# Second products of the attention scores and the filter features over 128 partitions instead of 64

## The chip, the cores and the metric

The kernel runs on one core of a Trainium2 chip. The time is device microseconds of one execution; several executions were timed, and one more view of an execution, the profile, tells what each engine did and when. Engines are named as the profile names them: PE is TensorE's matmul, PEld its weight load, DVE VectorE, ACT ScalarE, POOL GpSimd, SP SyncE, which here issues all DMAs.

## What is computed

One layer of a two-branch encoder over two inputs, the prompt (1024 tokens) and the sample (512 tokens), both 1024 channels wide:

```python
def encoder_layer(x, ...):
    h = rmsnorm(x, norm_g)
    z = h @ w_in
    ...
    # branch 1: long convolution with a filter that a small network makes
    hy_in = short_conv(hy_in, conv_w, conv_b)
    x0, x1, vv = jnp.split(hy_in, 3, axis=-1)
    kfilt = hyena_filter(L, f_w1, f_b1, f_fr1, f_w2, f_b2, f_fr2, f_w3)
    y_hy = x0 * long_conv(x1 * vv, kfilt, hy_bias)
    y_hy = rmsnorm(y_hy, on_hy) * jax.nn.silu(hy_gate)
    # branch 2: attention in a window of 8 rows by 16 columns of a grid 64 wide
    q = rmsnorm(q.reshape(B, L, N_HEADS, HEAD_DIM), qn_g)      # 8 heads of 64
    k = rmsnorm(k.reshape(B, L, N_HEADS, HEAD_DIM), kn_g)
    y_att = neighbourhood_attention(q, k, v, rpb)
    y_att = rmsnorm(y_att, on_att) * jax.nn.silu(att_gate)
    return x + jnp.concatenate([y_hy, y_att], axis=-1) @ w_out

def hyena_filter(L, w1, b1, fr1, w2, b2, fr2, w3):
    ...
    h = jnp.sin(fr1 * (z @ w1 + b1))
    h = jnp.sin(fr2 * (h @ w2 + b2))       # L x 64, the features
    h = h @ w3                              # 64 -> 1024 channels
    h = h * jnp.exp(-t01 * jnp.abs(deltas))
    ...
```

All is float32. TensorE works on a rounded form, so every exact operand is held as a rounded part (hi) and what is left (lo), and a product is made of hi x hi, hi x lo and lo x hi.

## The kernel before, in words

**Stages.** First the prompt's x is normed and turned channel-major (`x_norm`, `x_turn`), and the features of the filters are made (`filters_mlp`, L166 its matmuls). Then the prompt's q, k and v are projected (`qk_proj` and `v_proj`, matmuls at L405), and alongside `k_phase` makes the filters of both groups and transforms them (L568, L569, then L461 to L463). Then comes the prompt's long convolution (`hyena`, with projections at L392), then the attention of the prompt alongside the projections and the convolution of the sample, then the output product (`out_part`, L1111) alongside the attention of the sample, and last the rest of the outputs.

**Order.** Generators are woven step by step in a fixed plan, some with a priority; the order on each engine is then set by the scheduler of the language, which runs a timeline of its own over the program while it is built. Any edit can so move instructions far from it. Each engine takes its queue in order; all DMAs stand in one queue, SP's. Room is given out by pools. A pool that is closed hands its room to the next ones on the same side, and an instruction that writes there waits for the last reader of the tile before.

**Filter products.** A feature and its weight each have 64 values, so a tile of 128 partitions holds two sorts of them. `hm` (features) has, for direction d, hi on the partitions of d and lo on the other 64; `w3[d]` has hi of the weights on both halves. One matmul over 128 partitions (L568) therefore makes hi x hi + lo x hi. The missing hi x lo is a second matmul, over the 64 partitions of d alone (L569), against `w3[2]`, which holds lo of direction d on the partitions of d. Two such pairs fill a bank, and `k_phase` multiplies it by the decay `dec` (into `xk`, VectorE). `dec` is loaded through three buffers, three loads ahead.

**Scores.** Per pair of heads `load_pair` fills `kst` (k: hi on the head's half of the partitions, lo on the other), `qhh` (q: hi on both halves) and `qlo` (lo of q of the two heads, each on its half, in one tile). In `soft` L994 multiplies `qhh` by `kst` over 128 partitions, and L995 the head's half of `qlo` by the same half of `kst`, into the same bank. There are 64 such pairs for the prompt (half of them with 360 columns, half with 480) and 32 for the sample (360 columns). VectorE adds the table and finds the smallest (L998, `mx`), ScalarE takes exponentials (L1002), and the weights are scaled, turned (L1020) and multiplied by the values (L1029).

**Around it.** `issue_w` splits the weights into hi (L365) and lo (L366, on GpSimd). `gap` is a tile that is never used: it holds room free between the sample's projections and the pools of the sample's hyena, so that the first outputs (`ops0`, `ops1`, `acc0`, `first`) find room while that hyena still runs. `oo` (L1123, ScalarE) is the tile of the pool `first`, through which the outputs of the prompt's second half pass. W (copied at L671) is the spectrum of a block in `long_conv`.

Of the kernel before, what the change touches and what calls it, by code (L numbers as in the profile page):

```python
# [49 lines left out]
class Kernel:  # L50
# [6 lines left out]
    # ---------------------------------------------------------------- helpers  # L57
# [28 lines left out]
    def psum(self, side, keep=0, **banks):  # L86
        """Share the banks of one side out anew, but for its first keep pools: tag -> number of banks."""
# [11 lines left out]
    # ------------------------------------------------------------------ setup  # L99
    def setup(self):  # L100
# [27 lines left out]
        # DRAM scratch  # L128
# [11 lines left out]
    def mlp_setup(self, fl, mp):  # L140
        io = self.io
        self.hm, self.z, self.w12 = {}, {}, []
        self.w3 = [fl.tile([P, HW], F32R, name=f"w3{n}") for n in ("f", "b", "lo")]
# [12 lines left out]
    def filters_mlp(self, G, mp):  # L156
        nc = self.nc
        tag = "" if G.nseg > 1 else "_s"
        w1, w2 = self.w12
        h = self.z[G.name]  # L160
        for layer, (w, b, fr) in enumerate(((w1, "b1", "fr1"), (w2, "b2", "fr2"))):
            nxt = None if layer else mp.tile([P, G.L], F32, name=f"h1_{G.name}")
            for s in range(G.nseg):
# [3 lines left out]
                arg = mp.tile([P, 512], F32, name="arg" + tag, bufs=G.nseg)  # L167
                self.ts(arg, ps, self.v[b], ALU.add, self.v[fr], ALU.mult)
                n = mp.tile([P, 512], F32, name="n" + tag, bufs=G.nseg)
# [16 lines left out]
    def stack(self, out, src):  # L186
        """The halves of the partitions of src, split: hi in their own place and lo on the other half."""
        for d in range(2):
            r, o = slice(d * 64, d * 64 + 64), slice(64 - d * 64, 128 - d * 64)
            self.nc.scalar.copy(out=out[d][r], in_=src[r])  # L190
            self.sub(out[d][o], src[r], f32(out[d][r]))

    def w3_load(self, pool):
        """The last weights of the filters: per half of the partitions hi on both halves, and lo in its place."""
        raw = pool.tile([P, HW], F32, name="w3", bufs=1)
        self.dma(raw, self.io["w3"])
        for d in range(2):
# [3 lines left out]
            self.sub(self.w3[2][r], raw[r], f32(self.w3[d][r]))  # L201

    def rsqrt(self, pool, ss, n, scale, name):
        """(ss * scale + eps) ** -0.5 for a [P, n] tile."""
# [13 lines left out]
    # ------------------------------------------------------------ input norm  # L218
    def x_norm(self, G, xp, ahead):
        """The rows of x, scaled by their rms."""  # L220
# [18 lines left out]
    def x_turn(self, G, hps):  # L239
        """Channel-major copies of the normed x, split into hi and lo."""  # L240
# [12 lines left out]
    def x_pre(self, G, pool):  # L253
        """Channel-major copies of the normed x, split into hi and lo, to scratch."""
# [39 lines left out]
    # --------------------------------------------------------------- weights  # L294
    def steps(self, what):
        """The pieces of the weights that each step of a generator takes."""
# [19 lines left out]
    def merge(ns, spans):  # L316
        """The order in which generators of ns[i] steps take turns, each spread evenly over its span."""
# [3 lines left out]
    def plan(self, phases):  # L321
        """phases: lists of (names of chained generators, span, priority).  Sets the order of the weights."""
# [9 lines left out]
    def weave(self, *gens):  # L332
        """Trace the generators of the next phase in turns."""
# [10 lines left out]
    def fetch_w(self):  # L344
        """Load the next [P, 1024] piece."""
# [8 lines left out]
    def issue_w(self):  # L354
        """Split the next piece into two units of (hi, lo) [P, 512]; the piece behind it is on its way."""
# [13 lines left out]
    def take_w(self, key):  # L369
        """The next unit of piece key; pieces behind it are fetched as far as there is room."""  # L370
# [8 lines left out]
    def proj_ch(self, G, *gis):  # L379
        """128 output channels of each granule of gis, channel-major: per granule a list of psum [P, 512].  # L380
        The granules take turns in each segment of tokens."""
# [13 lines left out]
    def proj_tok(self, gi, hi, lo, nt):  # L395
        """256 output columns, token-major, for nt (<=8) token tiles.  Returns list of psum [P, 4, 256]."""
# [12 lines left out]
    # ----------------------------------------------------------------- hyena  # L409
    def conv(self, out, pss, ci):  # L410
        """short convolution along the free axis; ci = channel block (0..11)."""
# [13 lines left out]
    def dft_load(self, t, src, pool, tag):  # L425
        """src (DRAM) -> t [P, n, 128], rounded, through the room of a tag of pool."""
# [4 lines left out]
    def dft_mats(self, pool, src, fs, stage, tags):  # L431
        """The class matrices of the 128-point transforms: per class ((cos hi, lo), (sin hi, lo)).
# [101 lines left out]
    def k_phase(self, fp, between):  # L534
# [20 lines left out]
        for _ in range(3):  # L555
            fetch()
# [845 lines left out]
```

## Time and profile before

| | us |
|---|---|
| median of 3 runs | 1100.63 |
| lowest, highest | 1098.63, 1104.17 |
| span of the profiled execution, first to last instruction | 1101.3 |
| PE busy in it | 1030.7 |
| DVE busy in it | 824.4 |
| ACT busy in it | 561.1 |
| POOL busy in it | 539.9 |

The profiled execution lies inside the range of the timed ones. Busy time is the time in which at least one instruction of the engine is under way. On PE the matmuls overlap, so a row's duration is longer than the distance to the next one; the distance between two starts tells what a matmul takes of the engine. A form `64*128 64x360` is a matmul over 64 partitions, with 128 columns of weights and 360 moving columns.

### The profile page before, as it was taken

How to read it: one execution, taken by the hardware profiler on the slowest of the kernel's cores; microseconds unless marked ns; L12 is line 12 of the kernel's file. 1: busy time of each engine (PE TensorE's matmuls, PEld its weight loads, DVE VectorE, ACT ScalarE, POOL GpSimd, SP SyncE). 2: the span in 40 equal slices, each digit the busy share in tenths (PEclk: the TensorE clock that was granted, in tenths of full speed). 3: DMA queues.
4: the chain of work that ended last, by engine and by line, in shares of the span. 5: the costliest groups of instructions: out<-in, count | busy, mean ns of one | idle time of the engine just before them, and what ended most of it. 6: DMA issues, size and time to landing. Idle time of an engine off the chain costs nothing. (4 is left out here: it accounts for less than half of the span.)

```text
span 1101.3 us, 18549 instructions
## 1 busy us (share of the span) xinstructions
PE 1030.7 (94%) x6492; PEld 895.6 (81%) x6492; DVE 824.4 (75%) x2098; ACT 561.1 (51%) x1223; POOL 539.9 (49%) x480
## 2 busy tenths in 40 slices
PE   3999898998999999999898999999999999899998
PEld 2888887987888878787786887888777798798898
DVE  5988679456148597868768898999886868966874
ACT  6644616444534343443425577667567764564530
POOL 2133636325245474545445645455455564766452
PEclk9999999899999999999999899999999999999999
DMA  9134461645612121122375244445544376966522
GB/s 343 34 122 144 143 207 61 219 150 164 224 39 74 46 79 54 50 72 77 118 227 173 78 129 146 120 141 182 140 129 138 114 243 190 321 203 205 164 76 89
DMA packets 110780, 154.87 MB, mean 141 GB/s; under 512 B 7793, under 2 KB 80315, under 8 KB 109919
## 3 DMA queue, kind: packets, MB, share of 16 engines
q1 hardware_dynamic: 110687, 153.69, 44.3%
q8 instruction: 51, 0.84, 0.3%
q14 instruction: 42, 0.34, 0.1%
HBM read 110.35 MB, written 43.32 MB: 140 GB/s over the span
## 5 line engine op out<-in xcount | busy, mean ns | idle before, releaser
L366 POOL TENSOR_TENSOR wlo<-wraw,whi 128x512 fp32r<-128x512 f32 x160 | 231.5, 1451 | 308.4 <-ACT whi L365 180.7
L392 PE MATMUL bank<-hThi_p,whi 128*128 128x512 f32 x320 | 125.2, 391 | 2.0 <-DVE cx L75 2.0
L392 PE MATMUL bank<-hTlo_p,whi 128*128 128x512 f32 x320 | 125.5, 392 | 0.0
L392 PE MATMUL bank<-hThi_p,wlo 128*128 128x512 f32 x320 | 125.4, 392 | 0.0
L405 PE MATMUL bank<-whi,hThi_p 128*128 128x256 f32 x384 | 110.4, 290 | 2.5 <-ACT qsq L849 2.0
L1111 PE MATMUL bank<-whi,hi 128*128 128x256 f32 x384 | 111.0, 291 | 0.8 <-ACT hi L1090 0.5
L405 PE MATMUL bank<-wlo,hThi_p 128*128 128x256 f32 x384 | 110.8, 291 | 0.0
L1111 PE MATMUL bank<-wlo,hi 128*128 128x256 f32 x384 | 110.0, 288 | 0.0
L1111 PE MATMUL bank<-whi,lo 128*128 128x256 f32 x384 | 109.5, 289 | 0.3 <-POOL lo L63 0.3
L405 PE MATMUL bank<-whi,hTlo_p 128*128 128x256 f32 x384 | 108.1, 289 | 0.0
L450 POOL TENSOR_TENSOR Z<-zc,Z 128x256 fp32r<-128x256 f32 x80 | 69.5, 878 | 49.2 <-ACT Z L449 36.2
L1002 ACT ACTIVATE s_sb<-s_sb,mx 128x360 f32<-128x360 f32 (+1 forms) x96 | 60.4, 629 | 63.6 <-DVE mx L998 63.0
L405 PEld LDWEIGHTS bank<-whi,hThi_p 128*128 128x128 f32 x384 | 74.2, 194 | 4.9 <-ACT qsq L849 2.4
L1111 PEld LDWEIGHTS bank<-whi,hi 128*128 128x128 f32 x384 | 73.4, 191 | 4.1 <-issue 2.1
L405 PEld LDWEIGHTS bank<-wlo,hThi_p 128*128 128x128 f32 x384 | 74.5, 194 | 1.6 <-issue 0.7
L1111 PEld LDWEIGHTS bank<-wlo,hi 128*128 128x128 f32 x384 | 73.6, 192 | 1.6 <-issue 1.6
L1111 PEld LDWEIGHTS bank<-whi,lo 128*128 128x128 f32 x384 | 73.1, 192 | 1.7 <-issue 1.1
L405 PEld LDWEIGHTS bank<-whi,hTlo_p 128*128 128x128 f32 x384 | 73.3, 194 | 1.2 <-issue 0.7
L392 PEld LDWEIGHTS bank<-hThi_p,whi 128*128 128x128 f32 x320 | 60.3, 188 | 14.0 <-DVE cx L75 2.4
L392 PEld LDWEIGHTS bank<-hTlo_p,whi 128*128 128x128 f32 x320 | 60.4, 189 | 11.3
L392 PEld LDWEIGHTS bank<-hThi_p,wlo 128*128 128x128 f32 x320 | 60.3, 188 | 11.3
L392 PE MATMUL bank<-hThi_s,whi 128*128 128x512 f32 x160 | 64.6, 407 | 4.4 <-DVE cvv L75 2.3
(292 smaller groups left out, 3108.4 us busy)
## 6 DMA issues: line engine op xcount, KB each, us to landing
wraw<-in_w_ch_dram SPq DMA_DIRECT2D x40, 512.0 KB
wraw<-in_w_tk_dram SPq DMA_DIRECT2D x24, 512.0 KB
wraw<-in_w_out_dram SPq DMA_DIRECT2D x16, 512.0 KB
V<-v_p SPq DMA_DIRECT2D x32, 240.0 KB
v_p<-vg SPq DMA_DIRECT2D x32, 160.0 KB
K_p<-Kw SPq DMA_DIRECT2D x4, 1088.0 KB
x<-in_x_prompt_dram SPq DMA_DIRECT2D x8, 512.0 KB
dec<-in_dec_p_dram SPq DMA_DIRECT2D x16, 256.0 KB
```

Of the source, the lines that this page charges most:

```text
L366: nc.gpsimd.tensor_tensor(out=lo, in0=r, in1=f32(hi), op=ALU.subtract)
L392: nc.tensor.matmul(ps, lhsT=w, rhs=h[s][:, k], start=(k == 0 and i == 0), stop=(k == KC - 1 and i == 2))
L405: nc.tensor.matmul(pss[t // 2][:, t % 2, :], lhsT=h[t // 4][:, k, t % 4 * P:(t % 4 + 1) * P], rhs=w, start=(k == 0 and i == 0 and t % 2 == ...
L450: nc.gpsimd.tensor_tensor(out=Z[:, 1, 0:2, :], in0=z, in1=f32(Z[:, 0, 0:2, :]), op=ALU.subtract)
L1002: nc.scalar.activation(out=s_sb[:, :n], in_=s_sb[:, :n], func=AF.Exp, bias=mx, scale=-1.0, accum_out=l)
L1111: nc.tensor.matmul(ps[:, j, :], lhsT=h[:, tok], rhs=w, start=(k == 0 and i == 0 and j == 0), stop=(k == 3 and i == 2 and j == 1))
```

## The change

The second matmul of each pair now runs over all 128 partitions. For the filters, lo of the weights has a tile for each direction, with lo on both halves, so that the second matmul makes hi x lo + lo x lo. For the scores, lo of q has a tile for each head, with zeros on the other head's half; these zeros are written once, when the attention opens, by GpSimd, and the tiles are used in turn. The room for the larger tiles is taken elsewhere: the tiles `arg` and `n` of the filters' network share two buffers where the prompt had two and the sample one more of each; `dec` has two buffers and is loaded two ahead; `gap` is 1024 columns smaller. The diff also takes out comments, which moves the line numbers by a few (L995 is L1001 after, L569 is L568, L1111 is L1117).

```diff
@@ mlp_setup
-        self.w3 = [fl.tile([P, HW], F32R, name=f"w3{n}") for n in ("f", "b", "lo")]
+        self.w3 = [fl.tile([P, HW], F32R, name=f"w3{n}") for n in ("f", "b", "lof", "lob")]
@@ filters_mlp
-        tag = "" if G.nseg > 1 else "_s"
...
-                arg = mp.tile([P, 512], F32, name="arg" + tag, bufs=G.nseg)
+                arg = mp.tile([P, 512], F32, name="arg", bufs=2)
...
-                n = mp.tile([P, 512], F32, name="n" + tag, bufs=G.nseg)
+                n = mp.tile([P, 512], F32, name="n", bufs=2)
@@ w3_load
-            self.sub(self.w3[2][r], raw[r], f32(self.w3[d][r]))
+            self.sub(self.w3[2 + d][r], raw[r], f32(self.w3[d][r]))
+            self.sub(self.w3[2 + d][o], raw[r], f32(self.w3[d][r]))
@@ k_phase
-                decs.append(fp.tile([P, 2, 256], F32, name="dec", bufs=3))
+                decs.append(fp.tile([P, 2, 256], F32, name="dec", bufs=2))
...
-        for _ in range(3):
+        for _ in range(2):
             fetch()
...
-                r = slice(d * 64, d * 64 + 64)
...
                     nc.tensor.matmul(ps[:, j], lhsT=hm, rhs=self.w3[d][:, cs], start=j == 0, stop=False)
-                    nc.tensor.matmul(ps[:, j], lhsT=hm[r], rhs=self.w3[2][r, cs], start=False, stop=j == 1)
+                    nc.tensor.matmul(ps[:, j], lhsT=hm, rhs=self.w3[2 + d][:, cs], start=False, stop=j == 1)
@@ attention
+        qlos = []
+        for e in range(2):
+            ts = [ap.tile([P, 512], F32R, name=f"qlo{e}{i}", bufs=1) for i in range(G.nseg + e)]
+            for t in ts:
+                nc.gpsimd.memset(f32(t[64 - e * 64:128 - e * 64]), 0.0)
+            qlos.append(itertools.cycle(ts))
@@ load_pair
-            qlo = [ap.tile([P, 512], F32R, name="qlo", bufs=G.nseg + 1) for _ in range(G.nseg)]
+            qlo = [[next(qlos[e]) for e in range(2)] for _ in range(G.nseg)]
...
-                    self.stt(dst[o] if nm == "k" else qlo[s][r], ps[r], gn[r], f32(dst[r]), ALU.subtract)
+                    self.stt(dst[o] if nm == "k" else qlo[s][e][r], ps[r], gn[r], f32(dst[r]), ALU.subtract)
@@ soft
-            r = slice(e * 64, e * 64 + 64)
...
                 nc.tensor.matmul(sp[:, :n], lhsT=qhh[sg][e][:, q0:q0 + P], rhs=kv, start=True, stop=False)
-                nc.tensor.matmul(sp[:, :n], lhsT=qlo[sg][r, q0:q0 + P], rhs=kv[r], start=False, stop=True)
+                nc.tensor.matmul(sp[:, :n], lhsT=qlo[sg][e][:, q0:q0 + P], rhs=kv, start=False, stop=True)
@@ run
-        gap.tile([P, 2944], F32, name="gap")
+        gap.tile([P, 1920], F32, name="gap")
```

GpSimd's queue where the prompt's attention opens (Ybd belongs to the sample's hyena, T and pt to the attention, wlo is the lo part of weights; numbers are those of buffers), in the changed kernel:

```order
L773 MEMSET Ybd_6431 128x1024
L908 MEMSET T0_6353 128x2x40
L908 MEMSET T1_6356 128x2x40
L923 MEMSET pt0_6359 120x2x128
L923 MEMSET pt1_6361 120x2x128
L930 MEMSET qlo00_6363 64x512
L930 MEMSET qlo01_6364 64x512
L930 MEMSET qlo10_6367 64x512
L930 MEMSET qlo11_6368 64x512
L930 MEMSET qlo12_6369 64x512
L366 TENSOR_TENSOR wlo_6967<-wraw_6664,whi_6966 128x512
```

Before, the clears of T and pt stood some rows ahead of that of Ybd, and the clear of Ybd was followed at once by the wlo of the same piece of weights; now five new clears stand between.

SP's queue at the first loads of `dec` (hT is scratch for the sample's x, k_p scratch for the prompt's k), before:

```order
L60 DMA hT_76<-hl 128x4x128
L60 DMA dec<-in_dec_p_dram 128x512
L60 DMA hT_77<-hl 128x4x128
L60 DMA dec<-in_dec_p_dram 128x512
L60 DMA hyb<-in_hy_bias_dram 1x128
L60 DMA dec<-in_dec_p_dram 128x512
L60 DMA k_p_96<-raw_810 128x8x256
L60 DMA dec<-in_dec_p_dram 128x512
```

and in the changed kernel:

```order
L60 DMA dec<-in_dec_p_dram 128x512
L60 DMA hT_76<-hl 128x4x128
L60 DMA dec<-in_dec_p_dram 128x512
L60 DMA hT_77<-hl 128x4x128
L60 DMA k_p_96<-raw_811 128x8x256
L60 DMA dec<-in_dec_p_dram 128x512 x2
L60 DMA hT_76<-px 128x4x128
```

The loads of `dec` still alternate with the same stores; the load of hyb (the bias) is no longer among them, and the last two loads of `dec` follow each other.

ScalarE's queue where the outputs begin (oo and W as above; Y is the sample's spectrum product, ya the attention's values, qkr a square of them), before:

```order
L671 COPY W_9790<-bank_9841 128x256
L1039 ACTIVATE qkr_10532<-ya_8754 128x512
L1033 COPY ya_8755<-bank_10552 64x8x32
L1123 ACTIVATE oo_10874<-bank_10849,rh_p_3517 128x256 x2
L1039 ACTIVATE qkr_10563<-ya_8755 128x512
L665 CAST Y_9888<-yA_9869 128x256
L1123 ACTIVATE oo_10903<-bank_10878,rh_p_3517 128x256 x2
L667 ACTIVATE Y_9888<-Y_9888 128x2x128
L671 COPY W_9790<-bank_9877 128x256
```

and in the changed kernel:

```order
L670 COPY W_9795<-bank_9882 128x256
L1039 COPY ya_8760<-bank_10557 64x8x32
L664 CAST Y_9926<-yA_9907 128x256
L1045 ACTIVATE qkr_10568<-ya_8760 128x512
L666 ACTIVATE Y_9926<-Y_9926 128x2x128
L670 COPY W_9795<-bank_9915 128x256
L1129 ACTIVATE oo_10883<-bank_10858,rh_p_3520 128x256 x2
L1129 ACTIVATE oo_10912<-bank_10887,rh_p_3520 128x256 x2
```

Three copies go into W of the last block. Before, the first two pairs of oo stood behind the first of them; now they stand behind the third, the last.

## Rows read from the trace of the kernel before

**Rows 1.** The page's first part: busy us, share of the span, instructions.

```profile
PE 1030.7 (94%) x6492; PEld 895.6 (81%) x6492; DVE 824.4 (75%) x2098; ACT 561.1 (51%) x1223; POOL 539.9 (49%) x480
```

**Rows 2.** By stretches: us, busy PE, PEld, DVE, ACT, POOL; PEclk, DMA share, GB/s.

```profile
60.00:260.00 200.00, 186.73 (x1339) 170.13 (x1338) 147.57 (x407) 90.38 (x236) 89.39 (x80) 0.98 0.47 152
...
595.00:885.00 290.00, 280.43 (x1684) 232.32 (x1683) 250.47 (x636) 196.21 (x411) 153.50 (x136) 0.99 0.45 133
885.00:1056.00 171.00, 162.74 (x1204) 147.75 (x1203) 127.54 (x318) 90.36 (x209) 106.53 (x101) 0.99 0.69 211
```

**Rows 3.** The waits of PE, longest in total first: us, times, longest.

```profile
PE bank L248 <- DVE x L79: 18.1, 1, 18.1
PE bank L462 <- POOL Z L450: 4.7, 6, 1.2
```

**Rows 4.** Timeline of PE, 61 to 64 us: start, us, instruction, form, count.

```profile
61.17 0.28 PE L405 MATMUL bank<-whi,hTlo_p 128*128 128x256 f32 x1
...
61.66 0.28 PE L405 MATMUL bank<-whi,hThi_p 128*128 128x256 f32 x1
61.77 0.28 PE L568 MATMUL bank<-w3f,hm_p 128*128 128x256 f32 x1
61.98 0.38 PE L569 MATMUL bank<-w3lo,hm_p 64*128 64x256 f32 x1
62.29 0.39 PE L568 MATMUL bank<-w3f,hm_p 128*128 128x256 f32 x1
62.61 0.38 PE L569 MATMUL bank<-w3lo,hm_p 64*128 64x256 f32 x1
```

**Rows 5.** Timeline of the weight loader, the same stretch.

```profile
61.66 0.19 PEld L568 LDWEIGHTS bank<-w3f,hm_p 128*128 128x128 f32 x1
61.98 0.18 PEld L569 LDWEIGHTS bank<-w3lo,hm_p 64*128 64x128 f32 x1
```

**Rows 6.** Timeline of PE, 806 to 812 us.

```profile
807.56 0.33 PE L994 MATMUL bank<-kst,qhh 128*128 128x360 f32 x1
807.83 0.43 PE L995 MATMUL bank<-kst,qlo 64*128 64x360 f32 x1
808.19 0.68 PE L1029 MATMUL bank<-pt,V 120*64 120x256 f32 x4
...
809.66 0.39 PE L392 MATMUL bank<-hThi_s,whi 128*128 128x512 f32 x1
809.89 0.39 PE L392 MATMUL bank<-hTlo_s,whi 128*128 128x512 f32 x1
```

**Rows 7.** Single lines, L995 and L569: ns min/median/max, starts, forms; waits.

```profile
L995 PE MATMUL bank<-kst,qlo x96: 423/431/666, 599.2 to 1052.8; 64*128 64x360 f32 x64, 64*128 64x480 f32 x32
...
  issue: 20.5, 91
...
L569 PE MATMUL bank<-w3lo,hm_p x32: 378/381/382, 62.0 to 153.7; 64*128 64x256 f32 x32
...
  DVE xk L63: 13.6, 10
```

**Rows 8.** By stretches, of L995 alone: us, busy PE, PEld; PEclk, DMA share, GB/s.

```profile
595.00:885.00 290.00, 29.18 (x64) 11.69 (x64) 0.99 0.45 133
```

**Rows 9.** By shorter stretches, columns as in rows 2.

```profile
705.00:760.00 55.00, 54.12 (x336) 45.73 (x336) 51.58 (x128) 36.74 (x83) 27.98 (x24) 1.00 0.44 130
...
930.00:950.00 20.00, 18.15 (x122) 15.67 (x122) 17.84 (x42) 12.75 (x31) 14.23 (x13) 0.93 1.03 307
```

**Rows 10.** Single tile, w3lo: one of the two subtractions that fill it.

```profile
L63 DVE TENSOR_TENSOR w3lo<-w,w3f x1: 682/682/682, 24.0 to 24.0; 64x512 fp32r<-64x512 f32 x1
```

**Rows 11.** GpSimd: a clear among the groups by line, and its timeline at 582 us.

```profile
L878 POOL MEMSET vg<- 40x512 f32 x2 | 1.0, 517 | 5.2 <-DVE whi L365 5.2
...
581.72 1.31 POOL L366 TENSOR_TENSOR wlo<-wraw,whi 128x512 fp32r<-128x512 f32 x1 [2.42 <-DVE rs_t L81]
```

**Rows 12.** Timeline of VectorE: a multiplication by dec; in brackets its wait.

```profile
80.75 0.69 DVE L63 TENSOR_TENSOR xk<-bank,dec 128x512 f32<-128x512 f32 x1 [2.01 <-DMA dec<-in_dec_p_dram]
```

**Rows 13.** Single lines, L1123 and L671: ns min/median/max, first and last start.

```profile
L1123 ACT ACTIVATE oo<-bank,rh_p x16: 453/467/477, 901.4 to 967.4; 128x256 f32<-128x256 f32 x16
...
L671 ACT COPY W<-bank x40: 349/372/392, 348.9 to 920.8; 128x256 f32<-128x256 f32 x40
```

## The prediction

> **What bounds the kernel now.** I read the page's first part first: TensorE (PE) is busy 94% of the span, VectorE (DVE) 75%, ScalarE and GpSimd about half [rows 1]. A busy PE is not yet a bound, since matmuls overlap each other in that count. So the second view is the one by stretches: in the stretch of the filters (60 to 260 us), in that of the prompt's attention (595 to 885) and in that of the sample's attention (885 to 1056) PE is busy 93 to 97%, DVE 74%, 86% and 75% [rows 2]. The third view, who made PE wait, closes it: the one long wait (18.1 us) is the start, before the first transposes, and the next is already down to 4.7 us in six pieces [rows 3]. Behind the start PE hardly ever waits for anybody. What is left to find is how PE spends its own time, and that is read from the times at which one matmul starts after another.
>
> In the timeline four steps of full-height products of 256 columns take 61.66 - 61.17 = 0.49 us, 0.12 each. Then come the filter products: L568 starts 0.11 behind its predecessor, L569 (64 partitions) 0.21 behind L568, the next L568 0.31 behind that, the next L569 0.32 [rows 4]. The weight loads say why: the load for L568 starts at 61.66, 0.11 ahead of its matmul, while the matmul before it is running; the load for the 64-partition L569 starts at 61.98, with its matmul, and not under the one before [rows 5]. The change of height costs twice: the load into the short form waits for the running matmul, and so does the load back to the full form. The scores show the same: L994 to L995 0.27, L995 to the next 0.36 (360 columns), where full-height products of 512 columns follow each other in 0.23 [rows 6]. The weight loader stood 20.5 us before L995 alone, 91 times, with no engine named [rows 7].
>
> **The change part by part.** *Filter products.* A bank of q holds two pairs. Before: 0.21 + 0.31 + 0.32, and 0.31 to whatever follows (taken as in the pairs between) = 1.15 us. After, all four are full height: 4 x 0.12 = 0.48. So 0.67 for each of 24 banks (48 products: 32 of the prompt's features as the row says, 16 of the sample's by the loop) = 16 us of PE time [rows 4, 7]. VectorE waited 13.6 us for just these products [rows 7], so they lie on a path that others wait for. Against it stands the shorter look-ahead: dec has two buffers instead of three, so each load is issued one multiplication later. The trace has one wait of that kind, 2.01 us before the multiplication at 80.75 [rows 12]. Bounds: nothing, if the work that the new order places between covers it, and 2.01 for each of the 22 blocks that no longer start with a loaded buffer = 44 on VectorE, of which PE, three banks ahead, would feel a part. VectorE has 200 - 147.6 = 52 us free in that stretch [rows 2], so I take 2 us. Net 14.
>
> *Score products.* A full-height product of 360 columns lies between 0.12 (256 columns) and 0.23 (512): about 0.17. Pair before: 0.27 + 0.36 = 0.63; after 0.34. The saving is 0.29 at most, and 0.27 where L994 is short itself; for 480 columns the two extra steps are the same, as they are no streaming. I take 0.275 for each of 96 [rows 6, 7]: 64 pairs in the prompt's stretch [rows 8], 17.6 us, and 32 in the sample's, 8.8 us. What is late next? In the prompt's stretch VectorE works 250.5 of 290 us [rows 2]. Were all 17.6 kept, it would have to work 92% of 272. The busiest piece of this stretch, 705 to 760, has 51.58 of 55 = 94% with PE still at 54.12 [rows 9], so 92% is possible, but not over the whole stretch with a chain that passes from PE to VectorE, ScalarE and back. Bounds: 0 (VectorE keeps its present 86%) and 17.6 (94% would even allow 267 us). I take 90%, so 250.5 / 0.90 = 278: 12 us. In the sample's stretch VectorE has room (127.5 of 171), but the DMA queues are full for a part: a share of 1.03 in 930 to 950 with PE at 18.15 of 20 [rows 9]. What PE saves just there only waits for data. Bounds 0 and 8.8, taken 6.
>
> *What is added.* Two subtractions of 64x512 for the second pair of low halves of w3, 0.68 us each as their twins [rows 10], at 24 us where VectorE feeds the only long wait of PE: 1.4 us on the path. The filters' tiles arg and n, three sets before, share two: their steps follow each other on VectorE anyway, so the third segment finds a free set; taken 0, at most one step, 0.7. Eight clears of 64x512 on GpSimd: the 40x512 clear took 0.517 us [rows 11], so 5 x 0.52 = 2.6 us before the prompt's attention and 1.6 before the sample's. The order places the five directly behind the clear of Ybd and before the next wlo, where GpSimd stood 2.42 us waiting for VectorE [rows 11]; cover gone, they would delay wlo by 2.6. Taken 0. The doubled height itself I take at nothing: the products of full height are the quick ones in every row here.
>
> *What is moved.* The order of the stretches 60 to 260 and 560 to the end is dealt out anew; between them, some 250 us, it is row for row the same. One place is more than shuffling. gap has shrunk by 1024 columns, so the pool of oo lies on the room of the sample's hyena. In the new order of ScalarE the first two pairs of oo stand behind the last copy into W, where before only the first of three W copies stood ahead of them. In the trace oo began at 901.4, and the last W copy ran at 920.8 [rows 13]. Bounds: 0, as hyena's last block stands earlier on PE too, and 920.8 - 901.4 = 19.4 us, if the tail of hyena comes no sooner. Taken 2, near the lower end, since products of the other half of the outputs and hyena's own can run.
>
> *Sum.* 14 + 12 + 6 - 1.4 - 2 = 28.6. The profiled execution has a span of 1101.3 us; the three times run from 1098.63 to 1104.17 with a median of 1100.63, so nothing that lies around the span can be seen, and I take none. 1101.3 - 28.6 = 1072.7, against the median the same within 0.7: **1073 us**.
>
> **The rivals.** *VectorE takes over.* In the prompt's stretch the score products give nothing, and in the sample's the DMA takes the rest: only 16 - 2 + 0 - 1.4 = 12.6 stay, 1089 us. For it: the 86%; against: the 94% of one piece, and the few waits of PE.
>
> *No load goes under a full-height product of the same rows.* Then 128 partitions give the steps of 64 and the time stays 1101. The rows speak against it: the load at 61.66 is of the same full height as the matmul under way [rows 5]. The Trainium skill has this rule on its page "TensorE: Matmul & The Clock Gate", Part 3, "The mechanism": a weight load overlaps a running matmul only when it goes to other row groups. By that rule the change would bring nothing and cost 1.4 us. This trace disagrees, with 0.12 us a product for 256 columns over all rows. Only if something else than height held up the second product of a pair would the time come out so; that they share a bank is not it, for the products at 0.12 share one too.
>
> *The outputs wait for hyena (slower).* The two pairs of oo hold the banks of the first outputs until the tail of the sample's hyena is through, and PE, in order, stands there: 19.4 us. It decides from the point where this is more than what the products bring: with the 12.6 of the first rival the time is 1101.3 - 12.6 + 19.4 = 1108. With the gain of my forecast before the outputs it would still be 1101.3 - 28.6 + 17.4 = 1090. Against it: hyena's last products now stand ahead of the second group of outputs on PE.
>
> **How the numbers follow.** Forecast (between 20 and 42 us saved) 0.63; all the 42 and a little by luck of the order, 1056 to 1059, is its lower edge. VectorE takes over 0.18; outputs wait, with the gain kept (1090) 0.05 and with it lost (1108) 0.08; nothing changes 0.06. From below: 1101.3 - 16 - 17.6 - 8.8 = 1058.9, and I allow 3 us for the order: 1056. Above, the range reaches past the 1089 and 1090 cases to 1098, which leaves out the slower case and most of no change. A measurement of this kernel can tell about 0.5% (5.5 us). Faster than 1095.1: 0.63 + 0.18 + 0.05 less a little that falls short = 0.83. Within 0.5%: 0.06 and that little, 0.08. Slower: 0.09.
>
> **What would show it.** Right: the weight load of the second product starts under the first, L567 and L568 of the new kernel step at 0.12 us and the score pairs at about 0.17; "issue" is gone from the waits of the weight loader; the stretch to the end of the filters is some 13 us shorter, that of the prompt's attention some 12, with VectorE near 90% in it. Wrong: steps still of 0.3 us at those lines (second rival); VectorE's share unchanged in the attention, with new waits of PE for mx, pt or wlo (first); PE standing before the outputs, with oo behind W (third). A longer filter stretch with VectorE waiting for dec would refute my 2 us for the shorter look-ahead.

## The result and the profile after

| | median us | ratio to the kernel before | 95% interval |
|---|---|---|---|
| before | 1100.63 | | |
| changed | 1108.16 | 1.0072 | 1.0047 to 1.0096 |

0.7% slower, where 1073 us was predicted, in a range of 1056 to 1098. The profiled execution of the changed kernel has a span of 1103.2 us (it took 1105.0, 3 below the median). The page's first part and the view by stretches (columns as in rows 2), against [rows 1, 2]:

```profile
PE 993.2 (90%) x6492; PEld 897.0 (81%) x6492; DVE 832.6 (75%) x2100; ACT 559.7 (51%) x1223; POOL 536.8 (49%) x488
```

```profile
60.00:260.00 200.00, 184.47 (x1411) 176.37 (x1409) 144.10 (x399) 92.79 (x238) 84.39 (x79) 0.98 0.51 165
595.00:885.00 290.00, 264.02 (x1662) 233.29 (x1662) 252.48 (x622) 189.53 (x406) 146.11 (x131) 0.97 0.44 127
885.00:1056.00 171.00, 153.55 (x1193) 150.67 (x1192) 122.72 (x316) 92.56 (x208) 106.10 (x102) 0.95 0.69 213
```

PE is busy 37.5 us less (993.2 after 1030.7), and the span is no shorter: PE now stands. In 595 to 885 it gets through 1662 instructions where it got through 1684. The height did what it was to do. The timelines of PE and of the weight loader at the first filter bank, and the line L1001 (ns min/median/max), against [rows 4 to 7]:

```profile
61.10 0.28 PE L567 MATMUL bank<-w3f,hm_p 128*128 128x256 f32 x1
61.22 0.28 PE L568 MATMUL bank<-w3lof,hm_p 128*128 128x256 f32 x1
61.34 0.28 PE L567 MATMUL bank<-w3f,hm_p 128*128 128x256 f32 x1
```

```profile
61.10 0.19 PEld L568 LDWEIGHTS bank<-w3lof,hm_p 128*128 128x128 f32 x1
61.22 0.19 PEld L567 LDWEIGHTS bank<-w3f,hm_p 128*128 128x128 f32 x1
```

```profile
L1001 PE MATMUL bank<-kst,qlo x96: 321/332/502, 597.2 to 1054.1; 128*128 128x360 f32 x64, 128*128 128x480 f32 x32
```

Steps of 0.12 us where 0.21 to 0.32 stood, each load a step ahead of its matmul, 332 ns for 431, and "issue" gone from the waits of L1001. But the waits of PE, against [rows 3], have grown behind the start:

```profile
PE bank L248 <- DVE x L79: 18.5, 1, 18.5
PE bank L1000 <- DVE mx L1004: 10.5, 7, 4.9
PE bank L461 <- ACT Z L469: 6.4, 3, 4.8
PE bank L952 <- DVE mx L1004: 5.5, 3, 2.9
```

To put a sum on it I went through the starts of all matmuls of a trace. A step's own time is the median that its form, with that of the next matmul, has at full clock; what a step takes beyond it is put down as waiting, or, where the granted clock is at its lower level and the step is no more than about twice as long, as slow. In us:

| | own time | waiting | slow steps |
|---|---|---|---|
| before | 964.9 | 104.4 | 9.6 |
| all products 128, old order (e4 below) | 922.3 | 122.1 | 16.8 |
| changed | 920.8 | 143.1 | 16.4 |

So 44 us of PE's own time are gone, a little more than the 42.4 that the three products were priced at before their bounds; 39 came back as waiting and 7 as slow steps. The waits of PE that the profile itself lists behind the start say the same: they sum to 47.8 us before, 70.5 in e4 and 86.0 in the changed kernel. Two questions follow: why the height brings so little, and what makes the changed kernel worse than e4.

### The profile page after: what moved, and what is told of

It reads as the page before. It is cut to its first block, busy times and chain, and to the rows that moved or that the text cites. A ratio compares the mean times of both kernels' runs of the same rounds, so it can differ in the third digit from the quotient of the medians.

```text
span 1103.2 us, 18572 instructions
## 1 busy us (share of the span) xinstructions
PE 993.2 (90%) x6492; PEld 897.0 (81%) x6492; DVE 832.6 (75%) x2100; ACT 559.7 (51%) x1223; POOL 536.8 (49%) x488
## 4 chain that ended last, share of the span: by engine, by line
PE 44%; DVE 27%; DMA 13%; ACT 6%; issue 5%; POOL 4%; SPq 1%; DVEq 0%; POOLq 0%; ACTq 0%
PE bank L392 19%; PE bank L1117 9%; PE bank L405 4%; DMA v_p<-vg 2%; DMA qkr<-in_rpb_dram 2%; PE bank L1035 2%; DVE zc L63 2%; PE bank L462 2%; DVE whi L365 2%; PE bank L461 2%; PE bank L1026 2%; PE bank L463 2%; DMA dec<-in_dec_p_dram 1%; DVE rs_t L63 1%; SPq L60 1%
## 5 line engine op out<-in xcount | busy, mean ns | idle before, releaser
L366 POOL TENSOR_TENSOR wlo<-wraw,whi 128x512 fp32r<-128x512 f32 x160 | 228.9, 1434 | 288.6 <-ACT whi L365 159.3
L1117 PE MATMUL bank<-whi,hi 128*128 128x256 f32 x384 | 112.1, 293 | 5.0 <-DVE acc L75 2.6
L1117 PE MATMUL bank<-wlo,hi 128*128 128x256 f32 x384 | 111.4, 291 | 0.0
L1117 PE MATMUL bank<-whi,lo 128*128 128x256 f32 x384 | 110.2, 290 | 1.0 <-POOL lo L63 1.0
L450 POOL TENSOR_TENSOR Z<-zc,Z 128x256 fp32r<-128x256 f32 x80 | 68.3, 865 | 42.0 <-ACT Z L449 30.4
L1117 PEld LDWEIGHTS bank<-whi,hi 128*128 128x128 f32 x384 | 75.7, 197 | 6.1 <-DVE acc L75 3.3
L1117 PEld LDWEIGHTS bank<-whi,lo 128*128 128x128 f32 x384 | 75.0, 197 | 1.4 <-POOL lo L63 1.4
L1117 PEld LDWEIGHTS bank<-wlo,hi 128*128 128x128 f32 x384 | 75.8, 198 | 0.0
L1035 PE MATMUL bank<-pt,V 120*64 120x256 f32 (+1 forms) x352 | 67.8, 298 | 4.7 <-DVE pt L63 2.5
L365 DVE CAST whi<-wraw 128x512 fp32r<-128x512 f32 x94 | 60.5, 648 | 13.6 <-PE bank L392 5.9
```

What stands on the lines that cost most here:

```text
L365: next(self.w_round)(out=hi, in_=r)
L366: nc.gpsimd.tensor_tensor(out=lo, in0=r, in1=f32(hi), op=ALU.subtract)
L450: nc.gpsimd.tensor_tensor(out=Z[:, 1, 0:2, :], in0=z, in1=f32(Z[:, 0, 0:2, :]), op=ALU.subtract)
L1035: nc.tensor.matmul(o, lhsT=vl, rhs=pr_, start=(c == 0 and i == 0), stop=(c == ncu - 1 and i == 1))
L1117: nc.tensor.matmul(ps[:, j, :], lhsT=h[:, tok], rhs=w, start=(k == 0 and i == 0 and j == 0), stop=(k == 3 and i == 2 and j == 1))
```

## Experiments

**The height on either order.** The order that the scheduler makes does not depend on the height: on PE all 6492 rows of e1 stand as in the changed kernel, and those of e2 and e3 as in the kernel before. So the height can be changed with every row in its place (but for the sample's attention in e4, where a product now waits for both heads' low parts): back to 64 in the changed kernel (e1), and to 128 in the kernel before (e2 to e4), by giving the second products their full tiles:

```diff
 # e1, from the changed kernel: all its tiles, 64 partitions
-  lhsT=hm, rhs=self.w3[2 + d][:, cs]
+  lhsT=hm[d * 64:d * 64 + 64], rhs=self.w3[2 + d][d * 64:d * 64 + 64, cs]
-  lhsT=qlo[sg][e][:, q0:q0 + P], rhs=kv
+  lhsT=qlo[sg][e][e * 64:e * 64 + 64, q0:q0 + P], rhs=kv[e * 64:e * 64 + 64]
 # e2 (first pair), e3 (and the second for the prompt), e4 (for both), from the kernel before
-  lhsT=hm[r], rhs=self.w3[2][r, cs]
+  lhsT=hm, rhs=self.w3[2][:, cs]
-  lhsT=qlo[sg][r, q0:q0 + P], rhs=kv[r]
+  lhsT=qlo[sg][:, q0:q0 + P], rhs=kv
```

> The changed kernel with all its tiles, clears and loads, and with its order of instructions on every engine row for row, but both second products over 64 partitions again, as before. So the difference to the changed kernel (1108.2) is the height alone, on the new order. Theory A, the new room and order cost what the height gains: the height is worth its 28 to 37 us of TensorE time here too, so 1136 to 1145. Theory B, the other engines and their chain set the pace, and TensorE's saved time has nowhere to go: 1108 to 1116, hardly slower than the changed kernel. In between the share of each is read off: (this time - 1108.2) is what the height brings under the new order, (this time - 1100.6) what room and order cost under the old height.

> The kernel before, its order unchanged row for row on every engine, with only the filter product over 128 partitions (it multiplies the other direction's low halves as well, so the filters come out other than the reference's). It keeps three dec buffers. The step of the prediction says 16 us of TensorE time saved, 14 net with the shorter look-ahead that is not in here. Theory A: 1085 to 1088. Theory B: the VectorE multiplication that follows each bank sets the pace, 1095 to 1101.

> As the run with the filter product alone, and the prompt's score product over 128 partitions too (with the other head's low part of q and the low part of k in it, so the scores are not the reference's); order still that of before, row for row. Difference to the run with the filters alone is what the 64 score pairs of the prompt bring. Prediction: 12 us, bounds 0 and 17.6. Theory A: 1070 to 1076. Theory B, VectorE and the chain through mx, exponentials and weights set the pace in the prompt's attention: 0 to 4 us less than with the filters alone, 1083 or more.

> The kernel before with both second products over 128 partitions, the sample's scores too (scores and filters not the reference's, as in the other runs on the old order). Order as before up to the sample's attention (some 885 us); in it rows are dealt out anew, since a score product now waits for both heads' low parts of q. Prediction: 6 us less than with the prompt's scores. Theory A: 1064 to 1070. Theory B: within 2 us of the run with the prompt's scores; if the new deal of the sample's stretch costs by itself, slower than it.

| | median us | ratio to before | 95% interval |
|---|---|---|---|
| e1 | 1120.07 | 1.0197 | 1.0163 to 1.0232 |
| e2 | 1093.40 | 0.9936 | 0.9911 to 0.9960 |
| e3 | 1091.07 | 0.9923 | 0.9901 to 0.9945 |
| e4 | 1084.87 | 0.9868 | 0.9847 to 0.9888 |

Differences are taken from the ratios here and below, in us of 1100. The height is worth 14.5 us on the old order (e4) and 13.8 on the new one (1.0197 - 1.0072). By parts, on the old order: filters 7.0, the prompt's scores 1.4 (not told apart from nothing), the sample's scores, with the new deal of their stretch, 6.1. Neither theory held alone: the height is worth under half of what theory A said, and room and order cost 21.7 us at 64 partitions and 22.4 at 128. And e4 is faster than both kernels. It needs no tile, clear or smaller gap: what it adds to the sum is a product of two low parts that don't belong together, of the kind that the kernel before leaves out for its smallness.

**Which edit costs.** e5 is e4 with the gap alone, e6 e4 with the filter edits alone (w3lof and lob, dec two deep, arg and n shared), e7 with the score edits alone (a qlo tile per head, clears, gap). e9 is the changed kernel, and e10 e4, with oo on the other side (the pools opened after it on the old side move into its room):

```diff
 # e5
-  gap.tile([P, 2944], F32, name="gap")
+  gap.tile([P, 1920], F32, name="gap")
 # e9, e10
-  c, pools[n] = opn(n, "right")
+  c, pools[n] = opn(n, None if n == "first" else "right")
```

> The kernel with all products over 128 partitions in the old room (1084.9 us), with one edit of the changed kernel: gap has 1920 columns in place of 2944. The order of the engines is that of the 1084.9 kernel up to about 860 us. The changed kernel is 23 us slower than the 1084.9 one, and its trace loses them after 570 us. Theory G, the room: with the smaller gap the first outputs lie on room of the sample's hyena and wait for it: 1100 to 1108. Theory S, the scores' own tiles (one per head, used in turn, cleared by GpSimd): gap alone brings nothing, 1083 to 1088.

> The changed kernel with the filter part as it is (two tiles for the low halves of w3, dec with two buffers, arg and n shared), but the scores' low part of q in one tile for both heads, three buffers, no clears, and gap at 2944 as before; the second score product over 128 partitions reads both heads' low parts (the wrong head's low part meets the low part of k, a product of two low parts). Against the 1084.9 kernel this differs by the filter edits alone, which deal out the order anew from the start. Theory S or G (what costs lies in the scores' edits): 1083 to 1089, also with the 2 us of the shorter look-ahead. Theory L, every new order costs: 1092 to 1105.

> The other half: filters as in the 1084.9 kernel (one tile for the low halves, three dec buffers, own arg and n), the scores with all the edits of the changed kernel (a tile of q's low part per head, used in turn, clears, gap at 1920). Theory S or G: 1100 to 1108, nearly all of the 23 us. Theory L: between, 1092 to 1100. If it stays at 1085 to 1090, the filter edits or the two together are the cause.

> The changed kernel (1108.2 us) with one edit: the pool of oo is opened on the other side of the room, above the attention's pool, and so no longer on the room of the sample's hyena; gap stays at 1920. In the changed kernel oo starts at 910.4, right behind hyena's last copy into W at 910.2, and 123 output products stand by 920 us where the 1084.9 kernel has 256. Theory G as a wait for hyena's room: the time comes back to 1084 to 1090, with oo before 895. If the smaller gap does its harm in another way (another pool of the outputs, or the new order as such), 1100 to 1108.

> The 1084.9 kernel (all products over 128 partitions, gap 2944) with the pool of oo on the other side too. There oo had its room beside hyena already, from 889.7 on, 20 us ahead of hyena's last W copy. Theory G: nothing to gain, 1082 to 1088. If the room was a bound for the outputs even there, lower.

| | median us | ratio to before | 95% interval |
|---|---|---|---|
| e5 | 1105.52 | 1.0057 | 1.0032 to 1.0081 |
| e6 | 1085.06 | 0.9853 | 0.9820 to 0.9886 |
| e7 | 1106.76 | 1.0060 | 1.0034 to 1.0085 |
| e9 | 1111.97 | 1.0115 | 1.0084 to 1.0147 |
| e10 | 1093.72 | 0.9945 | 0.9926 to 0.9964 |

The filter edits cost nothing that shows (e6 is 1.7 us below e4, with intervals that meet). The gap alone costs 20.8 us, which looked like the wait for hyena's room. The line that writes oo, e4 ahead of e5:

```profile
L1123 ACT ACTIVATE oo<-bank,rh_p x16: 455/468/476, 889.7 to 953.3; 128x256 f32<-128x256 f32 x16
```

```profile
L1123 ACT ACTIVATE oo<-bank,rh_p x16: 456/467/483, 910.4 to 977.1; 128x256 f32<-128x256 f32 x16
```

ScalarE's timeline in e5 shows no wait for hyena at that place. The last copy into W is done by 901.0, and oo starts 9 us later, directly behind an exponential that stood for VectorE's minimum:

```profile
900.65 0.37 ACT L671 COPY W<-bank 128x256 f32<-128x256 f32 x1
...
909.67 0.59 ACT L1002 ACTIVATE s_sb<-s_sb,mx 128x360 f32<-128x360 f32 x1 [7.24 <-DVE mx L998]
910.17 0.19 ACT L1002 ACTIVATION_READ_ACCUMULATOR s_sb<-s_sb,mx 128x1 f32 x1
910.38 1.57 ACT L1123 ACTIVATE oo<-bank,rh_p 128x256 f32<-128x256 f32 x4
```

What held oo there was its place in ScalarE's queue. And e9 takes oo off that room, and is no faster (1.0115 against 1.0072). Its oo still starts late:

```profile
L1129 ACT ACTIVATE oo<-bank,rh_p x16: 455/471/480, 913.2 to 976.8; 128x256 f32<-128x256 f32 x16
```

That is 0.3 us behind the start of its last copy into W, as in the changed kernel: the place in ScalarE's queue stayed. But PE did not stand for it: among the waits of PE in the changed kernel's trace none is for oo.

And e10, which was to change nothing, lost 8.5 us (its five times run from 1087.45 to 1097.60, and its trace is of the quickest). Theory G, as a wait for hyena's room, fell for the changed kernel.

The orders show what the runs have in common. On PE, e6 has the order of e4 in the last 73% of its rows: only the filters' stretch is dealt anew. e7 has another order from the opening of the prompt's attention on, e5 and e10 from the outputs at some 890 us on; up to there they are 2.5 and 1.8 us ahead of e4.

**The clears, and the order alone.** e13 adds five clears to e4, e14 takes them from e1. e17 and e18 change no instruction and no tile of e4, only what the scheduler goes by:

```diff
 # e13, where pt is cleared
+  if big:
+      for i in range(5):
+          t = pts[i % 2].rearrange("p a b c q -> p (a b c q)")
+          nc.gpsimd.memset(f32(t[0:64, i // 2 * 512:i // 2 * 512 + 512]), 0.0)
 # e14
-  for t in ts:
-      nc.gpsimd.memset(f32(t[64 - e * 64:128 - e * 64]), 0.0)
 # e17
-  (["qk", "v", "ga"], (0.0, 1.1), 0)
+  (["qk", "v", "ga"], (0.0, 1.1), 1)
 # e18
-  for s in range(G.nseg) for nm in "kq"]
+  for s in range(G.nseg) for nm in "qk"]
```

> The 1084.9 kernel (products over 128 partitions, old tiles, gap 2944) with five more clears of 64x512 on GpSimd at the opening of the prompt's attention, written into the tiles pt that are cleared there anyway; nothing else. From the first output product of the prompt's convolution to the last projection of the sample the changed kernel takes 329 us where the 1084.9 kernel takes 309. Theory C, the clears (by delay or by the order that they bring): 1098 to 1106. Theory T, the tiles per head: 1084 to 1089, the 2.8 us of GpSimd's time at most.

> The changed kernel with both products over 64 partitions (1120.1 us) and without the clears, which that height does not need: tiles per head used in turn, gap 1920, dec with two buffers. Theory C: 1100 to 1108, with the stretch of the prompt's attention back at 313 us from 331. Theory T: 1115 to 1121. If the gap holds the outputs here as well, the end stays late even where the attention's stretch is short again, 1112 to 1118.

> The 1084.9 kernel with the same instructions and tiles; the priority of the sample's projections in the stretch of the prompt's attention is 1 in place of 0 (the others there have 5000). The order is the same up to the opening of the attention (some 565 us) and another from there on. Theory L, an order dealt anew loses by itself, since the old one is one that was picked: 1092 to 1106. Theory E, each edit had a price of its own: 1082 to 1088.

> The 1084.9 kernel with the same instructions and tiles; the pieces of a pair of heads are filled in the sequence q, k in place of k, q, which deals out the order anew from the opening of the prompt's attention. Theory L: 1092 to 1106. Theory E: 1082 to 1088.

| | median us | ratio to before | 95% interval |
|---|---|---|---|
| e13 | 1099.64 | 1.0000 | 0.9983 to 1.0018 |
| e14 | 1116.91 | 1.0145 | 1.0112 to 1.0179 |
| e17 | 1103.99 | 1.0026 | 1.0008 to 1.0044 |
| e18 | 1104.13 | 1.0018 | 0.9995 to 1.0042 |

The clears take 2.7 us of GpSimd and cost 14.5, as theory C had it; taking them out gains 5.7, with intervals that meet (e14 against e1), as theory T had it. The order alone is enough: the same instructions with a priority of 1 for 0 cost 17.4 us, with q filled before k 16.5, both in the range of theory L. So a new deal of the attention can cost by itself most of the 22.4 us between e4 and the changed kernel. The changed kernel's order is another deal, and how its 22.4 divide was not measured.

By the sums of above, e17 and e18 have the own time of e4 (922.1 and 922.3) and wait 139.2 and 133.0 us, with 17.6 and 24.1 of slow steps. Where it shows: the output products done in 860 to 920 us (busy PE, PEld; PEclk, DMA share, GB/s), in e4, in the changed kernel and in e17:

```profile
860.00:920.00 60.00, 35.55 (x256) 32.61 (x256) 1.00 0.62 192
```

```profile
860.00:920.00 60.00, 18.90 (x123) 17.53 (x123) 0.94 0.53 162
```

```profile
860.00:920.00 60.00, 15.58 (x105) 13.96 (x106) 0.83 0.56 175
```

In the last two, under half as many outputs stand between the last pieces of hyena and attention. That is a mark of the delay and not its measure: e18 has 167 there and e13 221, and they lose nearly as much as e17. Nor is one place common to the losses. By the sums of above, taken by stretches, e5 loses some 14 us more than e4 in 890 to 920, e17 some 9 in 870 to 890, e13 some 8 in 740 to 830.

**Where the height's time goes.** Three tries to free what PE waits for: e8, e4 with every second whi rounded on ScalarE; e11 and e12, 64 and 128 rows of the filter product without the loads of dec; e15 and e16, without and with the prompt's scores at 128, VectorE relieved.

```diff
 # e8, from the prompt's attention on
-  self.w_round = itertools.repeat(self.nc.vector.tensor_copy)
+  self.w_round = itertools.cycle([self.nc.vector.tensor_copy, self.nc.scalar.copy])
 # e11, e12: three tiles, loaded once, taken in turn
-  decs.append(fp.tile([P, 2, 256], F32, name="dec", bufs=3))
-  self.dma(decs[-1], ...)
+  if len(kept) < 3:
+      kept.append(fp.tile([P, 2, 256], F32, name=f"dec{len(kept)}", bufs=1))
+      self.dma(kept[-1], ...)
+  decs.append(kept[(24 - len(loads) - 1) % 3])
 # e15, e16
-  self.ts(s_sb[:, :n], s_sb[:, :n], rl)
+  self.ts(s_sb[:, :60], s_sb[:, :60], rl)
-  self.add(dst, yv[64:128], dst)
+  if G.nseg == 1:
+      self.add(dst, yv[64:128], dst)
```

> The 1084.9 kernel with every second rounding of the weights (whi) moved from VectorE to ScalarE from the prompt's attention on. 52 such casts of 588 ns are 30.5 us of VectorE's 252 in 595 to 885 us; half of them moved brings VectorE from 87% to about 82% and ScalarE from 70 to 75%. Theory B, VectorE sets the pace where the prompt's score products were to bring 12 us and brought 1 to 2: 1074 to 1081. If another thing holds that stretch (the clock, the chain from engine to engine), 1083 to 1088, or slower since ScalarE's own chain gets longer.

> The kernel before with the loads of the decay left out after the first three: the 24 multiplications take the first three tiles in turn, so the filters are not the reference's, and nobody waits for dec. The one to compare the next run with: the order of the two is the same row for row. In the kernel before only one wait for dec stood, 2.0 us, so 1094 to 1101 unless the order, which is dealt out anew against it, moves it.

> The same without the loads of the decay, with the filter product over 128 partitions. With the loads, the height of the filter product brought 6 to 7 us of its 16: VectorE's 13.6 us of waits for it shrank to 1.4, but 9.5 us of waits for dec stood in their place. Theory D, the late loads take the rest: 11 to 15 us below the run with 64 partitions and no loads. If something else holds that stretch (ScalarE's and GpSimd's share of the transforms, or the slower clock, 12 us of losses at half clock), 5 to 8 below it again.

> The kernel before with the filter product over 128 partitions, and VectorE relieved in the attention: the scaling of every second block of weights works on 60 columns in place of 360 or 480, and in the prompt's attention the addition of the low part of the values' product is left out (so the outputs are not the reference's). By the rows of the kernel before this takes about 18 + 13 of VectorE's 250 us in 595 to 885. The one to compare the next run with; the order of the two is the same row for row. Of itself 1080 to 1095, with the order dealt out anew.

> The same with the prompt's 64 score products over 128 partitions too. Without the relief this step brought 1.4 to 2.3 us of its 17.6. Theory B, VectorE's work is what the stretch is bound by: 8 to 15 us less than the run before. If the passing from engine to engine (scores, minimum, exponentials, weights) or the clock holds it, 1 to 5 us less again.

| | median us | ratio to before | 95% interval |
|---|---|---|---|
| e8 | 1098.23 | 0.9992 | 0.9973 to 1.0011 |
| e11 | 1122.33 | 1.0202 | 1.0184 to 1.0221 |
| e12 | 1110.84 | 1.0104 | 1.0077 to 1.0131 |
| e15 | 1104.74 | 1.0047 | 1.0025 to 1.0068 |
| e16 | 1101.51 | 1.0022 | 1.0004 to 1.0040 |

e8, e11 and e15 are slower than what they were made from, though less work is in their way: their order is a new one too. e11's is new on PE in the filters' stretch alone, with the last 74% of the rows as in the kernel before; it is 23 us behind that kernel at 300 us and 20 at the end. So a new deal of the filters, which cost nothing in e6, came with as large a loss here as one of the attention. e8 says nothing on VectorE; the pairs can be read within themselves, as each has one order.

*Filters.* Height brought 7.0 us with the loads and 10.8 without, just short of the 11 to 15 of theory D. The waits of VectorE in 60 to 262 us of e2, where the kernel before waited 13.6 us for these products [rows 7] and once, 2.0, for dec [rows 12]:

```profile
DVE xk L63 <- DMA dec<-in_dec_p_dram: 7.4, 6, 4.2
DVE xk L63 <- DMA dec<-in_dec_s_dram: 2.1, 1, 2.1
DVE xk L63 <- PE bank L569: 1.4, 1, 1.4
```

A load that was in time for the slow products is late for the quick ones. That takes part of the 16 us; the pair without loads waits more for the products at 64 rows (20.9 us on its order), so how much exactly stays open. How the rest divides was not measured. ScalarE's deliveries and the clock have a part in it: in 60 to 262 us PE's wait for ScalarE's Z (L469) grew from 2.6 to 6.2 us, that for its squares (L849) from 2.0 to 6.2; that for GpSimd's Z (L450) did not grow (3.9 and 2.3). The largest single wait of e2 there: PE stands before a projection for ScalarE's squares. The timeline of PE, and the stretches around it (columns as in rows 2):

```profile
93.22 0.58 PE L405 MATMUL bank<-whi,hThi_p 128*128 128x256 f32 x1 [6.15 <-ACT qsq L849]
93.60 0.41 PE L405 MATMUL bank<-wlo,hThi_p 128*128 128x256 f32 x1
```

```profile
80.00:86.80 6.80, 6.65 (x57) 6.45 (x55) 2.42 (x5) 0.76 (x2) 1.39 (x2) 1.00 0.88 267
86.80:93.20 6.40, 0.27 (x3) 0.06 (x1) 5.75 (x11) 1.85 (x5) 0.00 (x0) 0.72 0.56 190
89.60:96.50 6.90, 3.28 (x15) 3.28 (x16) 6.90 (x23) 4.95 (x11) 1.23 (x1) 0.51 0.13 43
96.50:104.00 7.50, 7.50 (x65) 7.50 (x64) 7.50 (x16) 3.67 (x11) 3.71 (x5) 1.00 0.56 144
```

*Prompt's scores.* e15 to e16 is 2.8 us, with intervals that meet, and with VectorE at 81% of 595 to 885 in e16 (235.0 of 290 us; 253.0 in e3):

```profile
595.00:885.00 290.00, 268.34 (x1686) 239.93 (x1687) 235.00 (x611) 194.03 (x420) 150.47 (x138) 0.95 0.44 131
```

Theory B, which had 8 to 15 us, fell: VectorE's share is not what holds this stretch. Where the saving goes can be followed from e2 to e3, on one order row for row: the steps of PE that got shorter sum to 24.8 us, those that got longer to 21.8, so the lead grew by 3. The waits of PE in 560 to 885 us, e2 and then e3:

```profile
PE bank L945 <- DVE mx L998: 1.9, 2, 1.2
PE bank L994 <- DVE mx L998: 1.8, 3, 0.9
PE bank L1020 <- DVE pt L63: 0.9, 2, 0.5
PE bank L763 <- DVE s L63: 0.6, 1, 0.6
```

```profile
PE bank L994 <- DVE mx L998: 4.8, 4, 1.5
PE bank L945 <- DVE mx L998: 2.7, 3, 1.2
PE bank L1020 <- DVE pt L63: 2.4, 3, 1.4
PE bank L763 <- DVE s L63: 2.0, 1, 2.0
```

These four grow from 5.2 to 11.9 us, and all that the view lists there from 12.7 to 25.6. So much of what is saved at a score is waited for at the next instructions in PE's queue that need the minimum, the weights or the sum of a transform. PE's rows come in one order in both runs, so what stands behind a waiting row waits too. The reading that fits is that these deliveries come when their own chain, through PE, VectorE and ScalarE in turn, has come round; no run shortened that chain as a whole.

## Why the prediction was wrong, point by point

- *What the products take.* Right: 0.12 us a step for the filters and 0.17 for scores of 360 columns, loads under the running matmul, 44 us of own time gone for the 42.4 priced. The second rival falls, and with it, here, the rule that it took from the Trainium skill's page "TensorE: Matmul & The Clock Gate", Part 3, "The mechanism": the loads at 61.10 and 61.22 go under a running matmul of the same rows.
- *What of it reaches the end.* Wrong: 14 + 2, 12 and 6 were taken, 7.0, 1.4 and 6.1 came (the 6.1 with a new deal of that stretch, so that it agrees may be luck). Two steps failed here. For the filters all of PE's 16 us was taken to reach the end, less 2 for dec; VectorE's waits for these products did shrink, from 13.6 to 1.4 us, but waits for dec and for ScalarE stood in their place. For the prompt's scores it is "I take 90%": it made a bound out of an engine's busy share.
  The first rival had the size for them (nothing) and its sign came, VectorE at 87% with new waits of PE for mx, but not the cause: with VectorE at 81% it was 2.8 us. Under both lies "Behind the start PE hardly ever waits for anybody" [rows 3]. The waits listed there are short, but they sum to 47.8 us, and they showed deliveries just in time where slack was read.
- *dec and w3lo.* 2 + 1.4 us were taken; e6 shows no cost of the filter edits, but its interval is 3.6 us to either side, so 3.4 is not excluded. Where dec hurts is at the quick products: VectorE waits 9.5 us for it in e2, with three buffers, and 11.0 in the changed kernel, with two, for 2.0 before.
- *Clears at nothing, moved steps at nothing but one.* Wrong, and the larger error: this is the step by which the forecast of a gain became a loss. "The order of the stretches 60 to 260 and 560 to the end is dealt out anew" stands in the text, with 3 us at the edge of the range for it and 2 for oo. (The five clears stand behind those of T and pt, and not directly behind that of Ybd.) Room and order together cost 21.7 us (64 partitions) and 22.4 (128), and a new order of the attention alone 16.5 and 17.4.
- *oo behind W.* Seen rightly in the order: in the changed kernel oo begins at 910.4, 0.3 behind the start of the last W copy. The gap alone cost 20.8 us where the bound said 19.4, but in e5 oo stood behind an exponential and not behind W. e9 frees oo from that room and gains nothing, and the rival's sign, PE standing before the outputs, is not in the changed kernel's trace. So the room is not what makes it slow. The third rival's 1108 is the measured time only by accident.

Left open: why the new orders lose. All seven of them that touch e4 behind the opening of the attention (e5, e7, e8, e10, e13, e17, e18) came out 8 to 21 us above it and none below. Only e17 and e18 change nothing but the order; the others bring edits of their own. That the old order was kept because it was a quick one would explain it, and no run tests that. The traces show where PE waits in them, and no run shows a rule by which one could tell a good order ahead.

## What to carry to other kernels

Where a scheduler sets the order, an edit has two prices: its own, and that of the order that it brings. The second was larger here, and it can be measured by itself: by a neutral edit that only deals the order anew, and by changing the one thing on an unchanged order. That the busiest engine's waits are short does not mean that the others have slack: price a saving by who delivers next, not by a busy share. And look for the edit that leaves the program as it is: reading the other half of a tile that is there (e4) kept a gain that the larger tiles lost.

## What the runs showed of the hardware

A half-height product cost more than a full one: against 0.12 us, 0.21 to 0.32 by the steps at both sides of it. PE's savings cost clock. In e2 PE stands 6.15 us, and the granted clock falls to 0.51, 1.2 of 2.4 GHz, from 89.6 to 96.5 us while it starts again; the first two products then take 0.58 and 0.41 us, for 0.28 at full clock. Over whole executions the granted clock (median of the runs) falls with the height on either order, from 0.987 to 0.979 (e4) and from 0.977 (e1) to 0.971 (changed). In us it is not priced by single traces: the slow steps are 9.6 us before and 16.8 in e4, but some 11 in e6 and e10, of e4's height.
